# Opening of a decoder's first layer: four token tiles normed before the first projection, 512-token blocks, constants loaded later

## The chip, the cores and the metric

The kernel runs on one core of a Trainium2 chip. The metric is the device time of one execution in microseconds (us); lower is better. All arithmetic on the matrix engine that matters here is in a rounded 32-bit format (`float32r`): each operand is split into a high part and a low part, and a product is made of three matmuls (high by high, high by low, low by high).

## The reference

The reference is a two-layer decoder over 1024 tokens of width 1024. Layer 0 is gated linear attention followed by a squared-ReLU MLP; layer 1 is windowed attention with sinks and another MLP. What matters here is the opening of layer 0:

```python
def rmsnorm(x, g):
    y = x * lax.rsqrt(jnp.mean(x * x, axis=-1, keepdims=True) + EPS) * g

def gla_mixer(h, w_in, w_gk2, b_gk, g_onorm, w_out):
    proj = h @ w_in                       # q 512 | k 512 | v 1024 | gate 1024 | glr 16
    gk = log_sigmoid(glr @ w_gk2 + b_gk) / 16
    bcum = cumsum of gk inside chunks of 64 tokens
    q_t = q * exp(bcum); k_t = k * exp(-bcum); k_dec = k * exp(b_last - bcum)
    # per head (4 of them): causal product inside a chunk, running state between chunks,
    # norm, silu(gate), output projection
```

## The kernel before, in words

Tokens lie in eight tiles of 128 (`x0` to `x7`, 512 KB each), in two halves of four tiles. For each tile `scaled` (lines 169 to 179) squares it on ScalarE with a running sum, makes the reciprocal root of the mean (`rstd_of`, lines 132 to 142: a Ln and an Exp on ScalarE, four small operations on VectorE) and multiplies tile, root and gain on VectorE. `turn_tile` (lines 184 to 197) transposes the result in eight 128x128 pieces on TensorE into two PSUM banks, and empties these in four pairs: ScalarE casts 256 columns to the high part (`hna_hi`, line 196), VectorE subtracts to get the low part (`hna_lo`, line 197). `norm_tile` is both.

The opening for head 0 (lines 229 to 394) does the following. The loads go out on SyncE's queue in the order x0, the gain row `g_mix0`, x1, the two weight blocks of q and k (`wqk`), x2, x3, then the low-rank gate weights `glr_raw` and `gk2_raw`, the constants `b_gk` and `g_on`, and x4 to x7. The weight blocks, `glr_raw`, `gk2_raw` and x4 to x7 share three slots of one pool (`raw_block`), so a load waits until an earlier user of its slot is done. Tiles 0 and 1 are normed and turned, tiles 2 and 3 only scaled; then a loop goes over the tokens in four steps of 256: the gate projection (`glr_part`, lines 271 to 280), then for q and k by turns one tile of the next pair is turned and 24 matmuls of 256 columns are done (`qk_part`), and the pair after that is scaled. `Head.decay` (lines 294 to 313) makes the decay factors of one half out of the gate with one matmul, five exponentials or logarithms, a scan and four more VectorE operations; `q_out` and `k_out` apply them to the PSUM results of q and k. Then come the value and gate projection per tile (`vg_proj`, matmuls of 512 columns), the chunk products (`inner`), and the next heads.

Three constants of the second layer, `gq`, `gkv` and `sinks` (lines 982 to 987), and `neg_sinks` (line 1098) are written far down in the program but have no input to wait for. A scheduler orders each engine's instructions by a simulated timeline in which the order of the program is only a priority. An instruction whose inputs the simulation takes as ready is put early. On the chip each engine then takes its instructions in that fixed order. `tc.issue_after(i)` adds an edge of order only: what the block traces on the engine of `i` is queued behind `i` on that engine. Engines other than that of `i` get no edge.

Of the kernel before, what the change touches and what calls it, by code (L numbers as in the profile page):

```python
# [16 lines left out]
P = 128  # L17
# [34 lines left out]
def kernel(  # L52
# [35 lines left out]
    def raw_block(shape, name):  # L88
        return raws.tile(shape, F32, tag="raw", name=name)
# [10 lines left out]
    def bank(tag, name, shape=None):  # L100
        return psum.tile(shape or [P, HALF], F32, tag=tag, name=name)
# [67 lines left out]
    def scaled(h, gain, name):  # L169

        hs = act_block([P, D], f"{name}_hs")
        ss = stat(f"{name}_ss", 1)
        nc.scalar.activation(hs, h, AF.Square, accum_out=ss)
        r = rstd_of(ss, D, name)
        if gain is None:
            nc.scalar.activation(hs, h, AF.Copy, scale=r)
        else:
            last["scaled"] = nc.vector.scalar_tensor_tensor(hs, h, r, gain, ALU.mult, ALU.mult)
        return hs
# [44 lines left out]

    def x_load(t, alloc):
        x_in[t] = alloc([P, D], f"x{t}")
        nc.sync.dma_start(x_in[t], xv[t * P:(t + 1) * P, :])

    x_load(0, act_block)
    g_mix0 = gain_rows(ln_mix[0], "g_mix0")  # L230
    x_load(1, act_block)

    def x_norm(t):
        norm_tile(hn, t, x_in[t], g_mix0, "na")
# [2 lines left out]
        return [load_cols(w_in, c + h * P, c + (h + 1) * P, f"wqk{h}_{c}") for c in (0, 512)]  # L237

    raw_qk = qk_load(0)
    for t in range(2, 4):  # L240
        x_load(t, act_block)

    gla_ctx = ExitStack()
    small = gla_ctx.enter_context(tc.tile_pool(name="gla", bufs=3))
    glr_raw = raw_block([P, KD, 16], "glr_raw")
    nc.sync.dma_start(glr_raw, w_in[:, 3072:3088].rearrange("(k p) c -> p k c", p=P))
    glr_w = small.tile([P, KD, 32], F32R, name="glr_w", bufs=1)
    gk2_raw = raw_block([32, 512], "gk2_raw")
    for i in range(2):
        nc.sync.dma_start(gk2_raw[i * 16:(i + 1) * 16, :], a_w_gk2[0])  # L250
    gk2 = small.tile([P, 512], F32R, name="gk2", bufs=1)
    glrT = act_block([P, T], "glrT", F32R)
    b_gk = small.tile([P, GLA_HEADS], F32, name="b_gk", bufs=1)
    nc.sync.dma_start(b_gk, a_b_gk[0].rearrange("(h p) -> p h", p=P), allow_slow_non_contiguous=True)
    g_on = small.tile([P, 256], F32, name="g_on", bufs=1)
    nc.sync.dma_start(g_on, a_onorm[0].partition_broadcast(P))

    not_first = small.tile([P, HALF], U8, name="not_first", bufs=1)
    nc.gpsimd.memset(not_first, 1)
    nc.gpsimd.memset(not_first.rearrange("p (c j) -> p c j", j=CHUNK)[:, :, 0:1], 0)  # L260
# [96 lines left out]
    nc.gpsimd.memset(gk2[96:P, :].bitcast(F32), 0.0)  # L357
    nc.gpsimd.memset(glrT[96:P, :].bitcast(F32), 0.0)
    for t in range(4, NT):
        x_load(t, raw_block)  # L360
    x_norm(0)
    x_norm(1)
    nc.scalar.copy(glr_w[:, :, 0:16], glr_raw)
    nc.vector.tensor_sub(glr_w[:, :, 16:32], glr_raw, glr_w[:, :, 0:16].bitcast(F32))
    for r in (0, 32):
        nc.scalar.copy(gk2[r:r + 32, :], gk2_raw)
    nc.vector.tensor_sub(gk2[64:96, :], gk2_raw, gk2[0:32, :].bitcast(F32))
    head = Head(0)
    qkw = qk_split(0, raw_qk)
    hs = {t: scaled(x_in[t], g_mix0, f"na{t}") for t in (2, 3)}  # L370
    ps_qk = []
    for half in range(2):
        ps_qk.append([bank("mm", f"q0_{half}"), bank("sc", f"k0_{half}")])
        for i in range(2):
            c0, c1 = i * 256, (i + 1) * 256
            t = 4 * half + 2 * i + 2
            glr_part(half, c0, c1)
            if t == NT:
                head.decay(1)
            for j in range(2):  # L380
                if t + j < NT:
                    turn_tile(hn, t + j, hs[t + j], "na")
                qk_part(ps_qk[half][j], qkw[j], half, c0, c1)
            for j in range(2):
                if t + j + 2 < NT:
                    hs[t + j + 2] = scaled(x_in[t + j + 2], g_mix0, f"na{t + j + 2}")
            if t + 2 >= NT:
                g = (t + 2 - NT) // 2
                if g == 0:
                    head.decay(0)  # L390
                head.q_out(g, ps_qk[g][0])
                head.k_out(g, ps_qk[g][1])
    for w in qkw:
        wt.back(*w)

# [15 lines left out]
    for h in range(GLA_HEADS):  # L411
        qt, kt, kd = head.e
        ebl = head.ebl
        if h > 0:
# [4 lines left out]
                    fin(half, ps)  # L419
            for w in qkw:  # L420
                wt.back(*w)
        wvg = vg_weights(h)
        pair = "p (n e j) -> p n e j"
        qp = act_block([P, T], f"qp{h}", F32R)
        ql = act_block([P, T], f"ql{h}", F32R)
# [16 lines left out]
        if h + 1 < GLA_HEADS:  # L442
            head = Head(h + 1)
            for half in range(2):
                head.decay(half)
            qkw = qk_split(h + 1, qk_load(h + 1))
        else:
            wo = proj_weights(a_w_out[0], "wo", 0, 3, (0,))

# [18 lines left out]
        def inner(n, v, sg):  # L468
            e = slice(n * P, n * P + CHUNK)
            o = slice(n * P + CHUNK, (n + 1) * P)  # L470
            ps = bank("sc", f"at{h}_{n}", [P, P])
            matmul(ps[:, 0:CHUNK], lhsT=kt[:, n * P:(n + 1) * P], rhs=qt[:, e], start=True, stop=True)
            matmul(ps[0:CHUNK, CHUNK:P], lhsT=kd[:, e], rhs=qt[:, o], start=True, stop=True)
            matmul(ps[CHUNK:P, CHUNK:P], lhsT=kt[:, o], rhs=qt[:, o], start=True, stop=True)
            at = attn_sb[n % 2]
            nc.vector.copy_predicated(at, causal.bitcast(U32), ps)
            ah = small.tile([P, 2, P], F32R, tag="at", name=f"ah{h}_{n}", bufs=1)
            nc.scalar.copy(ah[:, 0], at)
            nc.vector.tensor_sub(ah[:, 1], at, ah[:, 0].bitcast(F32))
# [23 lines left out]
            nc.vector.scalar_tensor_tensor(o_out, po, r, sg, ALU.mult, ALU.mult)  # L503

        prev = vg_proj(0)
        kn = [act_block([P, NT, P], f"kn{h}_{i}", F32R) for i in range(2)]
# [38 lines left out]
    class Blocks:  # L545
# [35 lines left out]
        def second_half(self, units, hs):  # L581
# [37 lines left out]
            for p1, p2, hi, lo, r11, b12, t1, b22 in work:  # L619
# [2 lines left out]
                nc.scalar.copy(hi["t4"], p2)  # L622
                v.tensor_sub(lo["t4"], p2, hi["t4"].bitcast(F32))

    def mix_out(first, lhs_of, wo, res_of, gain, name, mlp, begun=()):
        nxt = first
        hs = {}
        for t in range(NT):
            if t < len(begun):
                ht = begun[t]  # L630
            else:
                ht = act_block([P, D], f"{name}h{t}")
                nc.sync.dma_start(ht, res_of(t))
            lhs = nxt
            if t + 1 < NT:
                nxt = lhs_of(t + 1)
            if t == 6:
                mlp.blocks.second_half([(0, 0)], hs)
            proj_tile(lhs, wo, ht, f"{name}{t}", (range(K_BEGUN, KD),) if t < len(begun) else K_ALL)
            nc.sync.dma_start(mlp.h_in[t * P:(t + 1) * P, :], ht)  # L640
# [338 lines left out]
    mix_out(og_first, og_split, wo, lambda t: xv[t * P:(t + 1) * P, :], g_mlp0, "op", mlp)  # L979


    gq = const.tile([P, KD, 1], F32, name="gq")
    nc.sync.dma_start(gq, ln_mix[1].rearrange("(k p o) -> p k o", p=P, o=1), allow_slow_non_contiguous=True)
    gkv = const.tile([P, KD, 1], F32, name="gkv")
    nc.sync.dma_start(gkv, kv_norm.rearrange("(k p o) -> p k o", p=P, o=1), allow_slow_non_contiguous=True)
    sinks = const.tile([P, HEADS, 1], F32, name="sinks")
    nc.sync.dma_start(sinks, b_sinks[0].rearrange("(h o) -> h o", o=1).partition_broadcast(P))

    def gained(w, c0, c1, g, name, alloc=wt_block):
        raw = load_cols(w, c0, c1, name)  # L990
# [104 lines left out]
    oT = [act_block([P, KD, P], f"oT{t}") for t in range(NT)]  # L1095

    neg_sinks = const.tile([P, HEADS, 1], F32, name="neg_sinks")
    nc.vector.tensor_scalar(neg_sinks, sinks, -1.0, None, ALU.mult)

    UNIT = 2  # L1100
    STEPS = NT * NT
# [217 lines left out]
```

## Time and profile before

| what | value |
|---|---|
| median of 3 runs | 2114.4 us (2110.25 to 2116.42) |
| the profiled execution, its own time | 2115.71 us |
| its span in the trace | 2114.0 us |
| mean granted TensorE clock over the span | 0.985 of full speed |
| TensorE matmul busy | 2007.2 us (95%) |
| VectorE / ScalarE / GpSimd busy | 1567.2 / 970.0 / 241.9 us |

PE is TensorE, PEld its weight loads, DVE is VectorE, ACT is ScalarE, POOL is GpSimd, SP is SyncE and SPq the DMA issues of its queue. Matmuls overlap each other in the pipe, so the pace of a run of matmuls is read from start to start, not from the duration of one. "Idle" is the time for which an engine stood still just before an instruction, and the name behind the arrow is what let it go on. About 1.7 us of the execution's time lie outside the span.

### The profile page before, as it was taken

How to read it: one execution, taken by the hardware profiler on the slowest of the kernel's cores; microseconds unless marked ns; L12 is line 12 of the kernel's file. 1: busy time of each engine (PE TensorE's matmuls, PEld its weight loads, DVE VectorE, ACT ScalarE, POOL GpSimd, SP SyncE). 2: the span in 40 equal slices, each digit the busy share in tenths (PEclk: the TensorE clock that was granted, in tenths of full speed). 3: DMA queues.
4: the chain of work that ended last, by engine and by line, in shares of the span. 5: the costliest groups of instructions: out<-in, count | busy, mean ns of one | idle time of the engine just before them, and what ended most of it. 6: DMA issues, size and time to landing. Idle time of an engine off the chain costs nothing. (4 is left out here: it accounts for less than half of the span.)

```text
span 2114.0 us, 27260 instructions
## 1 busy us (share of the span) xinstructions
PE 2007.2 (95%) x9498; PEld 1662.1 (79%) x9498; DVE 1567.2 (74%) x3075; ACT 970.0 (46%) x2104; POOL 241.9 (11%) x252
## 2 busy tenths in 40 slices
PE   5899999997999999999988999998999999999996
PEld 5788888886788888888876778777788888888885
DVE  5767766658877768877885788866877776877786
ACT  5534433435555544333345577744554454433333
POOL 2231322101000000000010334422000000000000
PEclk9999999998999999999999999999999999999999
DMA  5216211421665569955321111222456567955502
GB/s 146 60 35 86 60 40 31 132 88 50 215 203 193 179 235 379 337 191 207 111 74 56 36 31 46 101 80 70 140 196 203 199 204 283 412 216 209 189 11 100
DMA packets 176809, 308.26 MB, mean 146 GB/s; under 512 B 14176, under 2 KB 110592, under 8 KB 176672
## 3 DMA queue, kind: packets, MB, share of 16 engines
q1 hardware_dynamic: 176672, 306.52, 42.8%
q8 instruction: 75, 1.23, 0.2%
q14 instruction: 62, 0.51, 0.1%
HBM read 202.67 MB, written 103.81 MB: 145 GB/s over the span
## 5 line engine op out<-in xcount | busy, mean ns | idle before, releaser
L106 PE MATMUL dx<-dt,ds 128*128 128x512 f32 x672 | 154.9, 389 | 0.6 <-ACT dt L684 0.6
L106 PEld LDWEIGHTS dx<-dt,ds 128*128 128x128 f32 x672 | 125.9, 188 | 27.6 <-ACT dt L684 1.4
L875 DVE TENSOR_TENSOR hr<-hr,dx 128x512 f32<-128x512 f32 x160 | 107.9, 681 | 37.7 <-PE dx L106 37.2
L684 ACT CAST ds<-du 128x512 fp32r<-128x512 f32 x128 | 79.2, 619 | 119.7 <-PE dy L106 51.7
L684 ACT CAST s<-s 128x512 fp32r<-128x512 f32 x128 | 79.5, 621 | 101.3 <-PE ux L106 50.3
L685 DVE TENSOR_TENSOR s<-s,s 128x512 fp32r<-128x512 f32 x128 | 87.8, 689 | 48.4 <-ACT s L684 48.3
L684 ACT CAST db<-dw 128x512 fp32r<-128x512 f32 x96 | 55.7, 619 | 122.7 <-PE dx L106 46.5
L106 PE MATMUL vg<-wvg_hi,hna_hi 128*128 128x512 f32 x256 | 102.9, 402 | 5.4 <-DVE e L318 4.8
L106 PE MATMUL vg<-wvg_hi,hna_lo 128*128 128x512 f32 x256 | 101.9, 398 | 0.0
L106 PE MATMUL vg<-wvg_lo,hna_hi 128*128 128x512 f32 x256 | 101.5, 397 | 0.0
L685 DVE TENSOR_TENSOR ds<-du,ds 128x512 fp32r<-128x512 f32 x128 | 90.7, 710 | 7.9 <-ACT ds L684 7.9
L106 PE MATMUL ux<-hb_t4h,a 128*128 128x512 f32 x256 | 86.5, 399 | 8.0 <-DVE u L761 7.9
L106 PE MATMUL dz<-db,da 128*128 128x512 f32 x384 | 93.9, 389 | 0.0
L106 PE MATMUL uz<-hb_b21h,a 128*128 128x512 f32 x256 | 88.3, 407 | 4.1 <-DVE u L733 4.1
L684 ACT CAST a<-wu 128x512 fp32r<-128x512 f32 x96 | 58.8, 620 | 62.1 <-PE uy L106 46.1
L106 PE MATMUL uy<-hb_b22h,s 128*128 128x512 f32 x256 | 85.0, 389 | 0.0
L106 PE MATMUL ux<-hb_b11h,a 128*128 128x512 f32 x256 | 84.3, 390 | 0.0
L106 PE MATMUL uy<-hb_t1h,s 128*128 128x512 f32 x256 | 84.3, 390 | 0.0
L106 PEld LDWEIGHTS dz<-db,da 128*128 128x128 f32 x384 | 72.0, 188 | 15.3 <-DMA da<-uo 0.3
L106 PE MATMUL ux<-hb_t3h,s 128*128 128x512 f32 x256 | 84.0, 389 | 0.0
L106 PE MATMUL ux<-hb_t2h,s 128*128 128x512 f32 x256 | 84.0, 389 | 0.0
L106 PE MATMUL dx<-db,da 128*128 128x512 f32 x336 | 79.6, 389 | 0.0
(390 smaller groups left out, 5627.2 us busy)
## 6 DMA issues: line engine op xcount, KB each, us to landing
uo<-uo SPq DMA_DIRECT2D x96, 512.0 KB, 5.1
da<-uo SPq DMA_DIRECT2D x96, 512.0 KB, 6.4
wu<-in_w_up_dram SPq DMA_DIRECT2D x64, 512.0 KB, 4.6
dw<-in_w_down_dram SPq DMA_DIRECT2D x64, 512.0 KB, 5.5
du<-us SPq DMA_DIRECT2D x64, 512.0 KB, 7.0
us<-us SPq DMA_DIRECT2D x32, 512.0 KB, 2.7
us<-u SPq DMA_DIRECT2D x64, 256.0 KB, 5.4
wvg_raw<-in_a_w_in_dram SPq DMA_DIRECT2D x32, 256.0 KB, 3.0
```

The lines of the kernel that those rows point to most:

```text
L106: ins = nc.tensor.matmul(*args, **kw)
L684: nc.scalar.copy(op[:, 0], src)
L685: nc.vector.tensor_sub(op[:, 1], src, op[:, 0].bitcast(F32))
L875: nc.vector.tensor_add(h, h, ps)
```

## The change

It loads x0 to x3 before the two weight blocks, and puts x4 to x7 and the gate weights into the 36-slot pool of activations instead of the three slots; `b_gk` and `g_on` are loaded after x7. It norms and turns tiles 0 to 3 before the first projection; the casts of the gate weights and of the q and k weights stand behind the last Square of these four on ScalarE. The gate projection and q and k of head 0 are done 512 tokens at a time. After the projections of half 0 tiles 4 to 7 are normed, with the `gk2` casts behind the Square of tile 4, and the casts of the v and gate weights of every head stand behind the Square of tile 5. The q and k weights of the next heads are loaded behind x7 on SyncE's queue. The three constants of the second layer are loaded behind the first store of the output projection, and `neg_sinks` stands behind the last operation of the gated attention on VectorE.

```diff
-        nc.scalar.activation(hs, h, AF.Square, accum_out=ss)
+        last["square"] = nc.scalar.activation(hs, h, AF.Square, accum_out=ss)
...
     x_load(0, act_block)
     g_mix0 = gain_rows(ln_mix[0], "g_mix0")
-    x_load(1, act_block)
+    for t in range(1, 4):
+        x_load(t, act_block)
...
     raw_qk = qk_load(0)
-    for t in range(2, 4):
-        x_load(t, act_block)
...
-    glr_raw = raw_block([P, KD, 16], "glr_raw")
+    gl_raw = act_block([P, D], "gl_raw")
+    glr_raw, gk2_raw = gl_raw[:, 0:KD * 16].rearrange("p (k c) -> p k c", k=KD), gl_raw[:32, HALF:D]
...
     for t in range(4, NT):
-        x_load(t, raw_block)
-    x_norm(0)
-    x_norm(1)
-    nc.scalar.copy(glr_w[:, :, 0:16], glr_raw)
-    nc.vector.tensor_sub(glr_w[:, :, 16:32], glr_raw, glr_w[:, :, 0:16].bitcast(F32))
-    for r in (0, 32):
-        nc.scalar.copy(gk2[r:r + 32, :], gk2_raw)
-    nc.vector.tensor_sub(gk2[64:96, :], gk2_raw, gk2[0:32, :].bitcast(F32))
+        x_last = x_load(t, act_block)
+    b_gk = small.tile([P, GLA_HEADS], F32, name="b_gk", bufs=1)
+    nc.sync.dma_start(b_gk, a_b_gk[0].rearrange("(h p) -> p h", p=P), allow_slow_non_contiguous=True)
+    g_on = small.tile([P, 256], F32, name="g_on", bufs=1)
+    nc.sync.dma_start(g_on, a_onorm[0].partition_broadcast(P))
+    for t in range(2):
+        x_norm(t)
+    for t in range(2, 4):
+        x_norm(t)
+    with tc.issue_after(last["square"].ins):
+        nc.scalar.copy(glr_w[:, :, 0:16], glr_raw)
+        nc.vector.tensor_sub(glr_w[:, :, 16:32], glr_raw, glr_w[:, :, 0:16].bitcast(F32))
+        qkw = qk_split(0, raw_qk)
     head = Head(0)
-    qkw = qk_split(0, raw_qk)
-    hs = {t: scaled(x_in[t], g_mix0, f"na{t}") for t in (2, 3)}
     ps_qk = []
     for half in range(2):
+        glr_part(half, 0, HALF)
         ps_qk.append([bank("mm", f"q0_{half}"), bank("sc", f"k0_{half}")])
-        for i in range(2):
...
+        for ps, w in zip(ps_qk[half], qkw):
+            qk_part(ps, w, half, 0, HALF)
+        if half == 0:
+            for t in range(4, NT):
+                x_norm(t)
+                if t == 4:
+                    with tc.issue_after(last["square"].ins):
+                        for r in (0, 32):
+                            nc.scalar.copy(gk2[r:r + 32, :], gk2_raw)
+                        nc.vector.tensor_sub(gk2[64:96, :], gk2_raw, gk2[0:32, :].bitcast(F32))
+                if t == 5:
+                    square = last["square"]
+        head.decay(half)
+        head.q_out(half, ps_qk[half][0])
+        head.k_out(half, ps_qk[half][1])
...
-        wvg = vg_weights(h)
+        with tc.issue_after(square.ins):
+            wvg = vg_weights(h)
...
-            qkw = qk_split(h + 1, qk_load(h + 1))
+            with tc.issue_after(x_last.ins):
+                raw_next = qk_load(h + 1)
+            qkw = qk_split(h + 1, raw_next)
...
+            first_store.setdefault(name, nc.sync.dma_start(mlp.h_in[t * P:(t + 1) * P, :], ht))
...
+    with tc.issue_after(first_store["op"].ins):
+        gq = const.tile([P, KD, 1], F32, name="gq")
+        nc.sync.dma_start(gq, ln_mix[1].rearrange("(k p o) -> p k o", p=P, o=1), allow_slow_non_contiguous=True)
...
...
-    nc.vector.tensor_scalar(neg_sinks, sinks, -1.0, None, ALU.mult)
+    with tc.issue_after(last["gla"].ins):
+        nc.vector.tensor_scalar(neg_sinks, sinks, -1.0, None, ALU.mult)
```

## Rows read from the trace of the kernel before

**Rows 1.** The page's first part: busy time of each engine, its share of the span, and instructions.
```profile
PE 2007.2 (95%) x9498; PEld 1662.1 (79%) x9498; DVE 1567.2 (74%) x3075; ACT 970.0 (46%) x2104; POOL 241.9 (11%) x252
```

**Rows 2.** The table by stretches: stretch (us from the span's start) and its length, busy time of PE, PEld, DVE, ACT and POOL with instructions in brackets, granted clock of TensorE, share of the DMA engines, GB/s.
```profile
0.00:23.00 23.00, 3.61 (x16) 3.14 (x16) 7.80 (x22) 11.71 (x25) 8.08 (x16) 1.00 0.84 239
23.00:54.00 31.00, 29.14 (x233) 27.34 (x232) 20.07 (x48) 18.12 (x48) 4.80 (x2) 1.00 0.27 81
...
54.50:58.50 4.00, 0.00 (x0) 0.00 (x0) 3.96 (x5) 3.11 (x8) 1.97 (x1) 1.00 0.03 10
58.50:64.00 5.50, 5.47 (x17) 4.34 (x18) 3.60 (x8) 1.58 (x4) 2.82 (x1) 0.69 0.93 258
...
76.00:115.00 39.00, 34.18 (x171) 27.90 (x171) 31.77 (x67) 20.70 (x54) 8.11 (x7) 0.91 0.09 28
...
98.00:112.00 14.00, 10.50 (x49) 8.32 (x48) 11.38 (x32) 4.94 (x18) 1.42 (x2) 0.76 0.00 1
...
115.00:200.00 85.00, 84.94 (x430) 70.45 (x429) 63.85 (x135) 33.50 (x94) 24.90 (x17) 1.00 0.45 75
...
400.00:500.00 100.00, 93.46 (x465) 78.68 (x464) 56.15 (x108) 41.92 (x101) 9.19 (x8) 0.97 0.26 85
```

**Rows 3.** The timeline of TensorE in the opening: start us, duration us, engine, line, operation, what it writes and reads, shape, count, and in brackets the idle time before it. `na_tp` are transposes of a normed tile, `glr_ps` the gate projection, `q` and `k` the projections, `vg` the value and gate projection.
```profile
21.33 1.94 PE L111 MATMUL na_tp<-ident,na_hs 128*128 128x128 f32 x8 [11.05 <-DVE na_v L136]
...
23.07 0.42 PE L106 MATMUL glr_ps<-hna_hi,glr_w 128*32 128x256 f32 x1
...
58.53 0.50 PE L106 MATMUL vg<-wvg_hi,hna_hi 128*128 128x512 f32 x1 [4.06 <-DVE e L318]
```

**Rows 4.** The timelines of ScalarE and VectorE between 9 and 20 us, same columns.
```profile
9.60 1.04 ACT L123 CAST wqk_hi<-wqk_raw 128x1024 fp32r<-128x1024 f32 x1 [3.35 <-DMA wqk_raw<-in_a_w_in_dram]
...
11.38 1.04 ACT L123 CAST wqk_hi<-wqk_raw 128x1024 fp32r<-128x1024 f32 x1 [0.47 <-DMA wqk_raw<-in_a_w_in_dram]
...
13.79 1.06 ACT L173 ACTIVATE na_hs<-x 128x1024 f32<-128x1024 f32 x1
...
17.34 0.17 DVE L1098 TENSOR_SCALAR neg_sinks<-sinks 128x16 f32<-128x16 f32 x1 [2.21 <-DMA sinks<-in_b_sinks_dram]
...
17.75 1.26 ACT L366 CAST gk<-gk_raw 32x512 fp32r<-32x512 f32 x2 [2.38 <-DMA gk_raw<-in_a_w_gk_dram]
19.03 0.20 ACT L138 ACTIVATE na_r<-na_r 128x1 f32<-128x1 f32 x1
```

**Rows 5.** The timeline of SyncE's queue: start, time that the issue held the queue, line, what is loaded.
```profile
11.02 0.89 SPq L983 DMA_DIRECT2D gq<-in_ln_mix_dram  x1
11.96 2.03 SPq L985 DMA_DIRECT2D gkv<-in_kv_norm_dram  x1
14.03 0.98 SPq L987 DMA_DIRECT2D sinks<-in_b_sinks_dram  x1
...
16.04 13.36 SPq L227 DMA_DIRECT2D x<-in_x_dram  x4
```

**Rows 6.** Groups of VectorE's, then of ScalarE's instructions in the first 60 us, by shape: busy us, mean ns of one, and idle time before them.
```profile
L178 DVE SCALAR_TENSOR_TENSOR na_hs<-x,na_r,g_mix 128x1024 f32<-128x1024 f32 x8 | 10.3, 1284 | 0.3
L197 DVE TENSOR_TENSOR hna_lo<-na_tp,hna_hi 128x256 fp32r<-128x256 f32 x25 | 10.2, 420 | 12.8 <-ACT hna_hi L196 12.7
L306 DVE TENSOR_TENSOR_SCAN e<-not_first,e 128x512 f32<-128x512 uint8 x1 | 1.2, 1225 | 0.0
L318 DVE SCALAR_TENSOR_TENSOR e<-q,e 128x512 f32<-128x512 f32 x1 | 0.7, 684 | 0.0
L196 ACT CAST hna_hi<-na_tp 128x256 fp32r<-128x256 f32 x26 | 9.3, 368 | 4.9 <-DVE hna_lo L197 3.2 <-PE na_tp L111 1.6
L173 ACT ACTIVATE na_hs<-x 128x1024 f32<-128x1024 f32 x8 | 8.4, 1052 | 2.4 <-DMA x<-in_x_dram 2.4
```

**Rows 7.** VectorE's small steps for tile 0 from the timeline: first row at which it starts, last at which the scaled tile begins; with the second and third row they are the four small steps of one tile.
```profile
5.62 0.15 DVE L136 TENSOR_SCALAR na_v<-na_ss 128x1 f32<-128x1 f32 x1 [5.62 <-ACT na_hs L173]
6.28 0.22 DVE L139 SCALAR_TENSOR_TENSOR na_t<-na_r,na_v 128x1 f32<-128x1 f32 x1 [0.51 <-ACT na_r L138]
6.53 0.15 DVE L140 TENSOR_SCALAR na_t<-na_t 128x1 f32<-128x1 f32 x1
6.71 0.16 DVE L141 TENSOR_TENSOR na_r<-na_r,na_t 128x1 f32<-128x1 f32 x1
```

**Rows 8.** Pace of TensorE, from its timeline, start to start: 256 columns (first and last of ten matmuls in a row), four transposes and what follows them, 512 columns of head 1 (first and last of eleven), and 512 columns at 60 us, two in a row.
```profile
28.04 0.28 PE L106 MATMUL q<-hna_lo,wqk_hi 128*128 128x256 f32 x1
...
29.11 0.28 PE L106 MATMUL q<-hna_lo,wqk_hi 128*128 128x256 f32 x1
...
51.57 0.60 PE L111 MATMUL na_tp<-ident,na_hs 128*128 128x128 f32 x4
51.93 0.36 PE L106 MATMUL k<-hna_hi,wqk_hi 128*128 128x256 f32 x1
...
150.17 0.39 PE L106 MATMUL mmqk<-hna_lo,wqk_hi 128*128 128x512 f32 x1
...
152.43 0.39 PE L106 MATMUL mmqk<-hna_hi,wqk_lo 128*128 128x512 f32 x1
...
60.26 0.63 PE L106 MATMUL vg<-wvg_hi,hna_hi 128*128 128x512 f32 x1
60.69 0.63 PE L106 MATMUL vg<-wvg_lo,hna_hi 128*128 128x512 f32 x1
```

More of the change, by code (lines that the diff above doesn't have):

```diff
@@ L226, in x_load @@
         x_in[t] = alloc([P, D], f"x{t}")
-        nc.sync.dma_start(x_in[t], xv[t * P:(t + 1) * P, :])
+        return nc.sync.dma_start(x_in[t], xv[t * P:(t + 1) * P, :])
     x_load(0, act_block)
     g_mix0 = gain_rows(ln_mix[0], "g_mix0")
-    x_load(1, act_block)
+    for t in range(1, 4):
+        x_load(t, act_block)
     def x_norm(t):
@@ L239 @@
     raw_qk = qk_load(0)
-    for t in range(2, 4):
-        x_load(t, act_block)
     gla_ctx = ExitStack()
     small = gla_ctx.enter_context(tc.tile_pool(name="gla", bufs=3))
-    glr_raw = raw_block([P, KD, 16], "glr_raw")
+    gl_raw = act_block([P, D], "gl_raw")
+    glr_raw, gk2_raw = gl_raw[:, 0:KD * 16].rearrange("p (k c) -> p k c", k=KD), gl_raw[:32, HALF:D]
     nc.sync.dma_start(glr_raw, w_in[:, 3072:3088].rearrange("(k p) c -> p k c", p=P))
     glr_w = small.tile([P, KD, 32], F32R, name="glr_w", bufs=1)
-    gk2_raw = raw_block([32, 512], "gk2_raw")
     for i in range(2):
@@ L252 @@
     glrT = act_block([P, T], "glrT", F32R)
[L253 to L256, printed above, removed]
     not_first = small.tile([P, HALF], U8, name="not_first", bufs=1)
@@ L371 @@
     ps_qk = []
     for half in range(2):
+        glr_part(half, 0, HALF)
         ps_qk.append([bank("mm", f"q0_{half}"), bank("sc", f"k0_{half}")])
-        for i in range(2):
[L375 to L392, printed above, removed]
+        for ps, w in zip(ps_qk[half], qkw):
+            qk_part(ps, w, half, 0, HALF)
@@ L502, in inner @@
             r = rstd_of(ss, 256, f"on{h}_{n}")
-            nc.vector.scalar_tensor_tensor(o_out, po, r, sg, ALU.mult, ALU.mult)
+            last["gla"] = nc.vector.scalar_tensor_tensor(o_out, po, r, sg, ALU.mult, ALU.mult)
         prev = vg_proj(0)
@@ L623, in second_half @@
                 v.tensor_sub(lo["t4"], p2, hi["t4"].bitcast(F32))
+    first_store = {}
     def mix_out(first, lhs_of, wo, res_of, gain, name, mlp, begun=()):
@@ L639, in mix_out @@
             proj_tile(lhs, wo, ht, f"{name}{t}", (range(K_BEGUN, KD),) if t < len(begun) else K_ALL)
-            nc.sync.dma_start(mlp.h_in[t * P:(t + 1) * P, :], ht)
+            first_store.setdefault(name, nc.sync.dma_start(mlp.h_in[t * P:(t + 1) * P, :], ht))
             hs[t] = scaled(ht, gain, f"{name}n{t}")
@@ L979 @@
     mix_out(og_first, og_split, wo, lambda t: xv[t * P:(t + 1) * P, :], g_mlp0, "op", mlp)
[L982 to L987, printed above, removed]
+    with tc.issue_after(first_store["op"].ins):
+        gq = const.tile([P, KD, 1], F32, name="gq")
+        nc.sync.dma_start(gq, ln_mix[1].rearrange("(k p o) -> p k o", p=P, o=1), allow_slow_non_contiguous=True)
+        gkv = const.tile([P, KD, 1], F32, name="gkv")
+        nc.sync.dma_start(gkv, kv_norm.rearrange("(k p o) -> p k o", p=P, o=1), allow_slow_non_contiguous=True)
+        sinks = const.tile([P, HEADS, 1], F32, name="sinks")
+        nc.sync.dma_start(sinks, b_sinks[0].rearrange("(h o) -> h o", o=1).partition_broadcast(P))
     def gained(w, c0, c1, g, name, alloc=wt_block):
```

## The prediction, as it was put on record

> **What bounds the kernel now.** I read the page's first part for the engine that carries the kernel, then the table by stretches for where that engine is not carried, then the timelines of those stretches. TensorE is busy 95% of the span [rows 1]. The table shows where the other 5% lie that this change can reach: from 115 to 200 us TensorE has next to no idle time, at full clock, but in the first 23 us it works 3.6 us, from 54.5 to 58.5 us not at all, and from 76 to 115 us it lacks 4.8 us [rows 2]. Behind the opening TensorE is full, so what is won or lost ahead of that point moves everything behind it by as much, at first sight to the end. The opening is therefore priced by when TensorE has done the same work.
>
> **Why the opening is slow.** The dense run starts at 23.07, after transposes of tile 1 that waited 11.05 us [rows 3]. The reader should see a queue in the wrong order. Tile 1 is squared only at 13.79, behind the casts of the q and k weights (the second at 11.38, let go by its load). Its Exp stands at 19.03 behind the `gk2` casts, for whose load ScalarE stood still 2.38 us; VectorE at the same time stood 2.21 us at `neg_sinks` for the load of `sinks` [rows 4]. SyncE's queue spends 3.9 us on `gq`, `gkv` and `sinks`, which nobody needs for hundreds of us, ahead of `gk2_raw` and x4, and the four last tiles then go out over 13.4 us as slots come free [rows 5].
>
> **The change part by part.**
>
> *Start of the dense run: 2.1 us earlier.* The five loads x0, `g_mix0`, x1, x2, x3 are now the first five. Before, the fourth and the fifth load released their readers at 9.60 and 11.38, 1.8 us apart [rows 4], so x3 is there at about 11.4. VectorE needs per tile the four small steps 0.68, the scaling 1.28 and four subtractions of 0.42, in all 3.64 us; ScalarE a Square of 1.05, its accumulator and Ln and Exp of 0.6, and four casts of 0.37, in all 3.1 us [rows 6, 7]. VectorE is the longer lane. It starts at 5.6 and has 2 us of work until tile 0 is turned at about 10. What then remains of four tiles is 14.6 - 2.0 = 12.6 us, so all is done at about 22.6. The projection can begin when the first of the last tile's four pieces is out, some 1.3 us earlier: 21.3, and I take 21.0, as such subtractions start closer than they last. Ends: 19.5 if VectorE is dense from 9 us, 24 if the Squares of x2 and x3 are put ahead of tile 0's casts and VectorE stands until 12.
>
> *Transposes already done: 1.4 us.* Tiles 2 and 3 are turned before the dense run instead of within it: 16 transposes at 0.36 us per four [rows 8].
>
> *512 columns instead of 256: 1.1 us.* 192 matmuls for q and k become 96. Ten of 256 columns take 1.07 us in nine steps, 0.119 each; ten steps of 512 columns 2.26 us, 0.226 each [rows 8]. 96 x (0.238 - 0.226) = 1.1 us; the gate projection I leave at nothing, bounded by the same 0.012 on its 32 pairs, 0.4 us. The Trainium skill, page "TensorE: Matmul & The Clock Gate", section "Back-to-back issue gap", puts a fixed 2.5 ns on top of the columns of each matmul; by it the term would be an estimated 0.24 us, as the loads of weights stand outside that formula. The rows decide.
>
> *Stalls inside the opening: 7.6 us.* Between 23 and 54 TensorE lacks 1.9 us, from 54.5 to 58.5 it lacks 4.06 (it waits for q's factors behind the late tiles 6 and 7), and in the 5.5 us behind that the granted clock is 0.69, a loss of 1.7 [rows 2, 3]; two matmuls there start 0.43 us apart against 0.226 [rows 8]. These follow from x4 to x7 coming late and in pieces [rows 5]; with them in the 36-slot pool they are issued at once and have landed by about 24 us, six large loads behind x3 at 1.8 us each, and the small ones. All three go, if tiles 4 to 7 are normed under the projections of half 0.
>
> *What comes in its place: 2.0 us lost.* Half 0 has 16 + 48 matmuls of 0.226, 14.5 us, and 32 transposes, 2.9 us, so TensorE is covered until 21.0 + 17.4 = 38.4. Tiles 4 to 7 take VectorE 14.6 us from 22.6, with 1.1 for gate results and weights: 38.3. That cover is just enough. If the scheduler puts the decay of half 0 between (a scan of 1.2, three operations of 0.68, one for q and two for k of 0.68, some 5.3 us in all [rows 6]), TensorE waits for tile 7. I take 1.5 of that, ends 0 and 5.3. The first 512-column matmuls run at half clock as the first 256-column ones do now (0.42 us for one against 0.28 [rows 3, 8]); with a little more work in that stretch I take 0.5, ends 0 and 1.7 (the loss at 58.5 us).
>
> *Edits at nothing.* The q and k weights land two loads later, at about 13 and 15 instead of 9.6 and 11.4 (two loads of 1.8 us); their split is needed only behind the gate projection, 3.6 us after the start. Were that cover gone, the price is the second split's lateness, at most 3 us. `b_gk` and `g_on` go behind x7 to some 26 us; the first decay is due later than that. The v and gate weights get their slots earlier than before. The three constants cost SyncE 3.9 us where the output projection stores its tiles [rows 5]. TensorE is short of work there anyway for 6.5 of 100 us [rows 2], SyncE has one load and one store per tile, and the constants have no reader for hundreds of us. Bounds: 0.5 us won, 3.9 lost. `neg_sinks` could hold VectorE for its load once more, 2.2 us as now [rows 4], but behind the gated attention VectorE has gaps. I take 0.
>
> *The stretch behind, 76 to 115 us: 0.* It loses 4.8 us idle and some 3.4 by clock (14 us at 0.76 [rows 2]). Its waits are for VectorE, with the decays of heads 0 and 1 heaped up. The new order moves half 0's decay ahead, but the same work of head 1 follows. I leave it, ends 8 us won (all goes) and 4 us lost.
>
> *Sum.* 2.1 + 1.4 + 1.1 + 7.6 - 2.0 = 10.2 us off. The profiled execution took 2115.7, its span 2114.0; that gives 2105.5. This execution lies 1.3 us above the median of the runs, so by the median it would be 2104.2. I say 2105. A measurement of this kernel can tell about 0.3%, 6.3 us, from no change: faster means under 2108.1, slower over 2120.7.
>
> **Rivals.**
>
> *The later stretch goes too.* With half 0's decay, q and k done some 20 us ahead of half 1's, VectorE has less heaped up at head 1, and the stall of 2.7 us with its half clock goes. For it: VectorE is busy only 20 of 31 us from 23 to 54, so there is room [rows 2]. Against it: the stall is a chain of state and chunk products, not the heap alone. Time: 2105 - 8 = 2097.
>
> *VectorE becomes the bound of the opening.* The two lanes have four tiles to do before anything starts and four more under half 0, and the casts and subtractions already wait for each other (12.7 us of VectorE's idle is for ScalarE's casts [rows 6]). The scheduler's order holds edges on ScalarE only; VectorE, SyncE and TensorE may be put otherwise than the program says, so that the change does not do all it says. With the start at 24 (3.0 lost), the full 5.3 us before tile 7 (3.8 more than taken), 1.2 more at half clock: 10.2 - 8.0 = 2.2 us off, 2113.5.
>
> *Slower: nothing overlaps between the halves.* TensorE now has no 256-token step to fall back on. If VectorE does decay, q and k of half 0 first and norms tiles 4 to 7 only then, half 0 ends at 24 + 15 = 39, the outputs at 41, tile 7 at 41 + 15 = 56, half 1 at 56 + 15 + 1.7 = 72.7. Before, that work less the 5.4 us of `vg` for tile 0, done in between, ended at about 70.5. So 2.2 us are lost, and if the heads behind inherit the order with another 4 us, 2122. It decides against the change from the point where tile 7 is turned later than 54 us. Against it: tiles 4 to 7 stand ahead of the decay in the program, and VectorE works only two thirds of this stretch today [rows 2].
>
> **How the numbers follow.** Forecast 0.52 (2100 to 2110), later stretch too 0.14, VectorE bound 0.22, slower 0.12. The range takes 2095 to 2115: the low end holds most of the first rival, the high end the whole of the second. Faster by over 0.3%: nearly all of the forecast's 0.52 (0.48) and the first rival, 0.62. Slower by over 0.3%: 0.09, the slower rival's upper part and mishaps far behind the opening. Same: 0.29.
>
> **What would show it.** In the changed profile: first gate projection at 21 (19.5 to 24) with four tiles turned; Squares of tiles 0 to 3 ahead of the weight casts on ScalarE; no wait for `gk2_raw` or `sinks` before 40 us; x7 issued before 20 us; q and k of half 1 done by about 56 to 58 us; no gap like that of 4.06 us. Wrong would be: a start after 24, a gap of more than 5 us between the two halves, a gap on TensorE near the constants' loads, or an order of heads 1 to 3 that loses more than 4 us where TensorE is full today.

## The result and the profile after

The changed kernel takes 2131.4 us (median; 2131.2 to 2134.2), beside 2113.9 for the kernel before on the same chip: a ratio of 1.009, interval 1.0076 to 1.0104. It is 17.5 us **slower**, where 2105 and "faster" were forecast. The profiled execution took 2134.2 us, its span 2132.5.

The table by stretches of the changed kernel, columns as in [rows 2]; the third and fifth stretch were not shown before.
```profile
0.00:23.00 23.00, 4.97 (x20) 3.85 (x20) 10.86 (x27) 13.66 (x32) 7.71 (x16) 1.00 0.93 291
23.00:54.00 31.00, 20.54 (x85) 14.91 (x85) 11.51 (x26) 11.30 (x26) 4.08 (x3) 0.94 0.11 32
46.00:72.00 26.00, 6.89 (x31) 5.14 (x30) 18.37 (x34) 14.78 (x34) 9.30 (x4) 0.58 0.28 81
54.00:76.00 22.00, 9.70 (x37) 7.66 (x38) 17.44 (x32) 9.83 (x26) 5.58 (x3) 0.54 0.31 94
76.00:115.00 39.00, 35.90 (x167) 27.98 (x166) 22.02 (x39) 18.84 (x38) 8.49 (x5) 0.91 0.09 27
115.00:200.00 85.00, 83.31 (x429) 69.23 (x427) 65.42 (x136) 33.58 (x93) 24.60 (x17) 1.00 0.31 51
```
Against [rows 2] TensorE has lost 8.6 us of work between 23 and 54 (29.14 to 20.54). A new hole stands between 46 and 72: 6.89 us of work in 26, at a granted clock of 0.58. Behind 76 us the stretches look as before. The last q and k matmul of head 3 starts at 320.55 before and at 338.25 after: at 320 us the whole loss (17.7) is there, and it is only carried on.

TensorE in the opening, columns as in [rows 3]:
```profile
15.99 1.94 PE L111 MATMUL na_tp<-ident,na_hs 128*128 128x128 f32 x8 [5.42 <-DVE na_v L136]
21.55 1.08 PE L111 MATMUL na_tp<-ident,na_hs 128*128 128x128 f32 x4 [3.61 <-DVE na_t L140]
26.07 2.28 PE L111 MATMUL na_tp<-ident,na_hs 128*128 128x128 f32 x8 [3.44 <-DVE hna_lo L197]
...
28.81 0.64 PE L106 MATMUL glr_ps<-hna_hi,glr_w 128*32 128x512 f32 x1 [0.46 <-ACT hna_hi L196]
...
46.11 0.40 PE L106 MATMUL k<-hna_hi,wqk_lo 128*128 128x512 f32 x1
46.35 0.60 PE L111 MATMUL na_tp<-ident,na_hs 128*128 128x128 f32 x4
...
58.45 1.94 PE L111 MATMUL na_tp<-ident,na_hs 128*128 128x128 f32 x8 [11.26 <-DVE na_v L136]
...
63.41 1.09 PE L111 MATMUL na_tp<-ident,na_hs 128*128 128x128 f32 x4 [3.03 <-DVE hna_lo L197]
...
70.41 2.02 PE L111 MATMUL na_tp<-ident,na_hs 128*128 128x128 f32 x8 [4.47 <-DVE hna_lo L197]
72.08 0.78 PE L106 MATMUL glr_ps<-hna_hi,glr_w 128*32 128x512 f32 x1
```
Two things are to be seen. The first gate projection starts at 28.81, not at 21.0 (at 23.07 before, [rows 3]). And half 0's last k matmul starts at 46.11, while tile 5 is turned at 58.45, tile 6 at 63.4 and tile 7 at 70.4: the second half of tile 4 and all of tiles 5 to 7 are turned behind half 0's projections, not under them. Half 1's first gate projection starts at 72.08.

ScalarE, same columns: the Squares (L173) and what stands ahead of them.
```profile
11.82 0.37 ACT L196 CAST hna_hi<-na_tp 128x256 fp32r<-128x256 f32 x1 [0.55 <-DVE hna_lo L197]
12.09 1.06 ACT L173 ACTIVATE na_hs<-x 128x1024 f32<-128x1024 f32 x1
...
17.52 1.99 ACT L123 CAST wqk_hi<-wqk_raw 128x1024 fp32r<-128x1024 f32 x2
19.41 0.64 ACT L196 CAST hna_hi<-na_tp 128x256 fp32r<-128x256 f32 x2
...
46.98 0.37 ACT L196 CAST hna_hi<-na_tp 128x256 fp32r<-128x256 f32 x1 [4.06 <-PE na_tp L111]
47.84 0.37 ACT L196 CAST hna_hi<-na_tp 128x256 fp32r<-128x256 f32 x1 [0.49 <-DVE hna_lo L197]
48.12 1.06 ACT L173 ACTIVATE na_hs<-x 128x1024 f32<-128x1024 f32 x1
...
49.16 2.92 ACT L123 CAST wvg_hi<-wvg_raw 128x1024 fp32r<-128x1024 f32 x3
```
The Square of x1 (12.09) stands behind the last cast of tile 0, and the Square of x5 (48.12) behind the last cast of tile 4. Tile 4's last casts wait for its transposes at 46.35, and those stand on TensorE behind half 0's last k matmul. So tile 5 is squared only when half 0 is done, and three v and g casts stand between its Square and its Ln.

VectorE in the changed kernel:
```profile
21.50 1.87 DVE L141 TENSOR_TENSOR na_r<-na_r,na_t 128x1 f32<-128x1 f32 x1
...
52.90 2.03 DVE L141 TENSOR_TENSOR na_r<-na_r,na_t 128x1 f32<-128x1 f32 x1
54.97 3.33 DVE L178 SCALAR_TENSOR_TENSOR na_hs<-x,na_r,g_mix 128x1024 f32<-128x1024 f32 x1
```
GpSimd at those times:
```profile
18.70 4.65 POOL L124 TENSOR_TENSOR wqk_lo<-wqk_raw,wqk_hi 128x1024 fp32r<-128x1024 f32 x2 [14.48 <-ACT wqk_hi L123]
50.27 6.94 POOL L124 TENSOR_TENSOR wvg_lo<-wvg_raw,wvg_hi 128x1024 fp32r<-128x1024 f32 x3 [26.92 <-ACT wvg_hi L123]
```
One small step takes 0.16 us in [rows 7] and 1.87 and 2.03 here, the scaling 1.28 in [rows 6] and 3.33 here. The step of 21.50 ends at 23.37, GpSimd's pair of subtractions at 23.35. In the hole this adds up: from the start of x5's Square (48.12) to the end of its scaling are 10.2 us, against 3.8 in a run where neither casts nor subtractions stand between (e2, 48.03 to 51.79; the same gap there is 4.84). So some 6.4 us of the first gap, 11.26, belong to the v and g casts and to GpSimd.

### The profile page after: what moved, and what is told of

The parts are those of the page before. It is cut to its first block, busy times and chain, and to the rows that moved or that the text cites. A ratio compares the mean times of both kernels' runs of the same rounds, so it can differ in the third digit from the quotient of the medians.

```text
span 2132.5 us, 26997 instructions
## 1 busy us (share of the span) xinstructions
PE 2013.4 (94%) x9370; PEld 1659.1 (78%) x9370; DVE 1571.5 (74%) x3073; ACT 969.0 (45%) x2100; POOL 241.2 (11%) x252
```

## The experiments

Each ran beside the kernel before on the same chip (2114 to 2116 us). The changed kernel has the ratio 1.009. Not all ran on one chip, so two rows are better compared by their ratios than by their medians, which can differ by 2 or 3 us on that account.

| kernel | us | ratio to before, interval |
|---|---|---|
| e1 Squares of tiles 4 to 7 ahead | 2127.9 | 1.0061, 1.0040 to 1.0083 |
| e2 v and g casts later | 2133.6 | 1.0094, 1.0074 to 1.0114 |
| e3 Squares of tiles 0 to 3 ahead | 2135.6 | 1.0099, 1.0081 to 1.0118 |
| e4 loads alone, on before | 2118.8 | 1.0018, 1.0009 to 1.0027 |
| e5 tiles 4 to 7 turned between | 2104.6 | 0.9956, 0.9944 to 0.9969 |
| e6 no low parts of weights | 2130.2 | 1.0080, 1.0055 to 1.0105 |
| e7 e4 with v and g held | 2113.3 | 1.0002, 0.9989 to 1.0014 |
| e8 constants alone, on before | 2112.3 | 0.9993, 0.9980 to 1.0006 |
| e9 e5 with the turning behind | 2114.7 | 1.0000, 0.9991 to 1.0009 |
| e10 turning between, alone | 2123.2 | 1.0042, 1.0026 to 1.0058 |
| e11 e5 with the first four too | 2103.3 | 0.9950, 0.9933 to 0.9967 |
| e12 e11 with the last four held | 2106.7 | 0.9962, 0.9950 to 0.9974 |

**e1, the Squares of tiles 4 to 7 ahead.**
```diff
             for t in range(4, NT):
-                x_norm(t)
+                hs[t] = scaled(x_in[t], g_mix0, f"na{t}")
...
+            with tc.issue_after(last["square"].ins):
+                for t in range(4, NT):
+                    turn_tile(hn, t, hs[t], "na")
```


> The changed kernel, but tiles 4 to 7 are all scaled before any of them is turned, and the casts of their turning stand behind the Square of x7 on ScalarE. Theory A (queue order: the Squares of x5 to x7 stand behind tile 4's casts, which wait for TensorE's transposes behind k of half 0): the hole from 47 to 70 us on TensorE closes for the most part, 12 to 18 us off the 2131.4 of the changed kernel, 2113 to 2119. Theory B (the hole is made by the three casts of the v and g weights and by GpSimd's subtractions, which hold VectorE): under 4 us off, 2127 to 2132, since both still stand behind the Square of x5.

2127.9. By the median that lies at the lower end of theory B's range (3.5 us off); by the ratios it is about 6 us off, between the two. The Squares of x5 to x7 came at 25.6, 30.5 and 37.6. But the v and g casts hang on the Square of x5 and came with it, and the dense run began only at 36.95. The hole stayed, smaller:
```profile
52.83 1.03 PE L111 MATMUL na_tp<-ident,na_hs 128*128 128x128 f32 x8
55.30 0.63 PE L111 MATMUL na_tp<-ident,na_hs 128*128 128x128 f32 x4 [1.20 <-DVE hna_lo L197]
...
58.20 1.09 PE L111 MATMUL na_tp<-ident,na_hs 128*128 128x128 f32 x4 [1.07 <-DVE hna_lo L197]
...
63.84 1.09 PE L111 MATMUL na_tp<-ident,na_hs 128*128 128x128 f32 x4 [3.02 <-DVE hna_lo L197]
```
These transposes had their scaled tiles by 43 us, yet they stand on TensorE behind half 0's last k matmul (52.60). From there each pair of transposes waits for the casts and subtractions of the pair ahead, with half 0's decay among them on VectorE, until 65.8. That made a new theory (D): what is exposed is the place of the turning in TensorE's own order.

**e2, the v and g casts later**, behind the Square of x7 in place of x5's (`if t == 7: square = last["square"]`).

> The changed kernel, but the casts of the v and g weights stand behind the Square of x7 instead of that of x5. Theory A: only the part of the hole that the casts and GpSimd's subtractions add goes: 2.9 us of casts between the Square and the Ln of x5, and 1.9 + 2.0 us by which VectorE's last small step and scaling of x5 outlast the same operations elsewhere (2.03 against 0.16, 3.33 against 1.28): 4 to 7 us off, 2124 to 2127.5. Theory B: most of the hole goes, 12 us or more off, under 2119.

2133.6: both missed, nothing is gained. Tile 5 is turned at 51.94 instead of 58.45, but the same casts and GpSimd's subtractions now fall among tiles 6 and 7, and the last wait is 7.96 us instead of 4.47.

**e3, the Squares of tiles 0 to 3 ahead.**
```diff
-    for t in range(2):
-        x_norm(t)
-    for t in range(2, 4):
-        x_norm(t)
+    hs = {t: scaled(x_in[t], g_mix0, f"na{t}") for t in range(4)}
+    with tc.issue_after(last["square"].ins):
+        for t in range(4):
+            turn_tile(hn, t, hs[t], "na")
```


> The changed kernel, but tiles 0 to 3 are all scaled before any is turned, and the casts of their turning stand behind the Square of x3. Theory A, applied to the start (the Square of x1 at 12.09 stands behind tile 0's casts although x1 is there at about 8): the first gate projection moves from 28.8 to 22 to 25 us, 4 to 7 us off, 2124 to 2127; the hole behind half 0 stays. Theory C (the start is bound by the work of ScalarE and VectorE on four tiles, whatever their order): within 2 us of 2131.4.

2135.6, no gain. Three tiles were scaled by 14.1, but then the casts of `glr_w` (which waited 1.22 us for its load) and of the q and k weights stood ahead of tile 0's later casts; the start came at 29.9 and the hole as before. What stands ahead had only changed its name.

**e4, the loads alone**: the kernel before with the changed order of loads, the input tiles in the 36-slot pool and the constants late; the 256-token steps kept.

> The kernel before with the loads of the change alone: x0 to x3 ahead of the weights, x4 to x7 and the gate weights in the 36-slot pool, the constants of both layers late; the steps of 256 tokens and the order of the norms stay. If the late loads made the stalls of the opening, as the prediction had it: 4 to 10 us off the 2113.9 of the kernel before, 2104 to 2110. If queue order made them: within 3 us of 2113.9.

2118.8: slower than before, outside both forecasts. x7 was issued by 14.3 and the gap of 4.06 of [rows 3] was gone, but the second transposes came at 23.71 and the dense run stuttered until 34.68. The v and g weights now came early too: their casts stood at 24.7, 27.0 and 28.8, GpSimd's subtractions from 25.8 to 32.8.

**e5, the turning between the quarters of half 0's projection**: the Squares as in e1, the v and g casts held behind tile 7's last cast.
```diff
-        for ps, w in zip(ps_qk[half], qkw):
-            qk_part(ps, w, half, 0, HALF)
...
+        pinned["PE"] = half == 0
+        for i, (ps, w) in enumerate(zip(ps_qk[half], qkw)):
+            for j in range(2):
+                qk_part(ps, w, half, 0, HALF, range(4 * j, 4 * j + 4))
+                if half == 0:
+                    turn_tile(hn, 4 + 2 * i + j, hs[4 + 2 * i + j], "na")
+        pinned["PE"] = False
+        if half == 0:
+            square = last["cast"]
```


> The changed kernel with tiles 4 to 7 all scaled before any of them is turned (as in e1), the turning of tiles 4, 5, 6 and 7 fixed on TensorE behind the first half of q, the second half of q, the first half of k and the second half of k of half 0, and the first head's v and g casts held behind the last cast of tile 7. In e1 TensorE finished half 0 at 52.6 and reached the first gate projection of half 1 at 65.8. Theory D (the order of TensorE puts the turning of tiles 4 to 7, sixteen casts and subtractions of about 0.86 us, behind half 0's projections): that gap shrinks to under 4 us, and with the start back at about 30 instead of 32 the time is 2112 to 2118. Theory C (ScalarE and VectorE have this much work wherever it stands, the opening is bound by them): the projection of half 0 is stretched by what the gap loses, 2124 to 2130.

2104.6, 7 us under the lower end of theory D and 26.9 better than the changed kernel (28 by the ratios); it beats the kernel before by 0.31 to 0.56%. Its table by stretches, then its TensorE:
```profile
23.00:54.00 31.00, 25.46 (x119) 18.00 (x120) 23.14 (x56) 16.45 (x47) 0.34 (x1) 1.00 0.10 30
54.00:76.00 22.00, 22.00 (x103) 16.84 (x102) 7.02 (x13) 12.02 (x20) 14.30 (x7) 1.00 0.50 144
76.00:115.00 39.00, 37.54 (x204) 31.34 (x203) 34.42 (x80) 19.00 (x58) 7.09 (x7) 1.00 0.00 1
...
98.00:112.00 14.00, 14.00 (x79) 11.91 (x78) 10.30 (x29) 5.18 (x21) 1.73 (x3) 1.00 0.00 1
```
```profile
30.59 0.78 PE L106 MATMUL glr_ps<-hna_hi,glr_w 128*32 128x512 f32 x1
...
39.37 1.03 PE L111 MATMUL na_tp<-ident,na_hs 128*128 128x128 f32 x8
...
50.36 0.39 PE L106 MATMUL k<-hna_hi,wqk_lo 128*128 128x512 f32 x1
51.09 0.63 PE L111 MATMUL na_tp<-ident,na_hs 128*128 128x128 f32 x4 [0.35 <-DVE hna_lo L197]
52.18 0.42 PE L106 MATMUL glr_ps<-hna_hi,glr_w 128*32 128x512 f32 x1 [0.46 <-ACT hna_hi L196]
```
Half 0's last k matmul starts at 50.36 and half 1's first gate projection at 52.18: 1.8 us between the halves, where the changed kernel has 26.0 (46.11 to 72.08). It starts 1.8 us later than the changed kernel and has half 1's last k matmul at 68.19 instead of 91.09. From 54 to 76 TensorE has no idle time, and its clock is full. Against the kernel before, though, the opening itself wins nothing: the last v and gate matmul of tile 3 starts at 98.35, before at 97.42. That of tile 7 starts at 126.50, before at 133.93. So what e5 has won by then, 7.4 us, it wins between these two points, where the kernel before works 10.50 of 14 us at a clock of 0.76 [rows 2] and e5 all 14.00 at full clock.

**e6, without the low parts of the first head's weights** (GpSimd's six subtractions left out, the high parts in their place).

> The changed kernel without GpSimd's six subtractions for the low parts of the first head's q, k, v and g weights (the high parts are used in their place, so the low parts are left out of the product; the matmuls stay as many). Theory E (while GpSimd subtracts 1024 columns, VectorE's operations from SBUF to SBUF are held, 0.16 us steps took 1.9 to 2.0 and a 1.28 us scaling 3.3): the first gate projection comes 2 to 3 us before 28.8 and tile 7 is turned 3 to 4 us sooner, 2124 to 2128. If what holds the tiles back is the order on ScalarE and TensorE alone: within 2 us of 2131.4.

2130.2, within 2 us of the changed kernel, as the second case had it; but the trace bears theory E out at the start. The first gate projection comes at 26.74 instead of 28.81, and the small step of tile 3 takes what it took in [rows 7] (its line is two further down here):
```profile
21.14 0.16 DVE L143 TENSOR_TENSOR na_r<-na_r,na_t 128x1 f32<-128x1 f32 x1
...
52.35 1.94 PE L111 MATMUL na_tp<-ident,na_hs 128*128 128x128 f32 x8 [7.35 <-DVE na_v L138]
62.96 1.94 PE L111 MATMUL na_tp<-ident,na_hs 128*128 128x128 f32 x8 [8.67 <-DVE hna_lo L199]
```
But the 2.1 us ahead run into the same hole. Tile 5 is turned after a gap of 7.35 instead of 11.26; then the next head's subtractions come in (GpSimd from 55.4 to 63.7), and tile 6 waits 8.67. So this run does not free the hole of subtractions, and what they cost there it does not tell.

**e7, e4 with the v and g casts held** behind tile 7's last cast.

> e4 (before, with the loads in the changed order, the input tiles in the activations' pool and the constants late; 256-token steps in the order of before) with the first head's v and g casts held behind the last cast of tile 7. e4 gave 2118.8 and had three of these casts and 7 us of GpSimd's subtractions between 24.7 and 32.8. Theory E and crowding (early loads let this work fall into the opening): 2110 to 2115. If the order of the Squares and weight casts (second transposes at 23.7) is what counts: within 2 us of 2118.8.

2113.3, 5.5 us better than e4 by the medians and 3.4 by the ratios, whose intervals overlap: the casts and subtractions that early loads had let into the opening are probably what e4 lost. The second transposes still came at 23.80, and against the kernel before nothing is gained (1.0002).

**e8, the constants alone**, on the kernel before.

> Before, with only the four constants of the second mixer (gq, gkv, sinks and their negative) loaded and worked out later. All theories: these do not sit on the path that sets the end, apart from 3 to 4 us of the SP queue ahead of input tiles 4 to 7 (11.02 to 16.04): 2111 to 2115, and not the place where the 17 us come from.

2112.3, no difference that can be told (0.9980 to 1.0006).

**e9, e5 with the turning put back** behind half 0's projection; Squares and held casts stay.

> e5 with the turning of tiles 4 to 7 put back behind half 0's last k matmul on TensorE; the Squares ahead and the v and g casts held behind tile 7's last cast stay as in e5. Theory D (the place of the turning on TensorE is what costs): sixteen casts and subtractions stand uncovered again behind half 0 (about 8 to 13 us), 2113 to 2120. If the held casts and the early Squares gave e5's 27 us: within 3 us of 2104.6.

2114.7, as theory D had it: 10.2 us more than e5, and the hole is back (half 0's last k matmul at 46.88):
```profile
47.11 1.03 PE L111 MATMUL na_tp<-ident,na_hs 128*128 128x128 f32 x8
...
54.02 1.09 PE L111 MATMUL na_tp<-ident,na_hs 128*128 128x128 f32 x4 [0.45 <-DVE hna_lo L197]
58.12 1.09 PE L111 MATMUL na_tp<-ident,na_hs 128*128 128x128 f32 x4 [3.02 <-DVE hna_lo L197]
...
60.12 0.78 PE L106 MATMUL glr_ps<-hna_hi,glr_w 128*32 128x512 f32 x1
```
From 47.1 to 60.1 are 13.0 us for sixteen casts with their subtractions. Not all of it is theirs: the wait of 3.02 is for VectorE, which does some 5.5 us of half 0's decay between 51.25 and 58.91.

**e10, the turning between alone**, with the Squares as in the changed kernel (the edit of e5 on TensorE's side, `x_norm(t)` in place of `turn_tile`).

> The changed kernel with the turning of tiles 4 to 7 fixed between the quarters of half 0's projection, and nothing else: Square x5 still stands behind tile 4's last cast on ScalarE and the v and g casts behind Square x5. Theory D alone: 2105 to 2112. If the place of the Squares counts as much (tile 5 is scaled only some 5 us after tile 4 is turned, and TensorE waits for it in the middle of q): 2115 to 2124. If neither: 2129 to 2133.

2123.2, the middle case: 8.2 us better than the changed kernel, and TensorE waits between q and k for tile 5:
```profile
51.12 1.94 PE L111 MATMUL na_tp<-ident,na_hs 128*128 128x128 f32 x8 [9.29 <-DVE na_v L136]
```
Its Square stands at 40.78, behind tile 4's last cast, but the scaling ends only at 50.97: here too the v and g casts and GpSimd's subtractions lie between, for 10.2 us instead of 3.8. The four kernels make a square: neither 2131.4, turning alone 2123.2, Squares and held casts alone (e9) 2114.7, both 2104.6. The two edits are worth 8.2 and 16.7 us each alone and 26.9 together (by the ratios some 10, 19 and 28). The second is itself two things. e1 has the Squares ahead without holding the casts (but for one edge of order on ScalarE) and takes 2127.9 against e9's 2114.7: with the Squares ahead, holding the casts is worth 13 us, and moving them alone (e2) nothing. Fixing TensorE's order for the turning fixes the gate projection ahead of q and q ahead of k as well; that was not tried apart.

**e11, e5 with the first four tiles done alike**: all Squares and scalings first, `glr_w` cast behind tile 1, the q and k weights behind tile 3, `gk2` behind the Square of x7.

> e5 with the same done for the first four tiles: all four Squares and scalings ahead of their casts, the cast of glr_w behind tile 1's last cast, those of the q and k weights behind tile 3's last, those of gk2 behind Square x7. In e5 the first gate projection came at 30.6, with VectorE's steps of tile 1 held from 21.5 to 23.4 while GpSimd subtracted q and k weights and two weight casts of 1 us ahead of tile 1's. If that order is what delays the start: it comes at 23 to 26 and the time is 2098 to 2101. If the sixteen casts and subtractions of 0.86 us bound the start in any order: 27 to 30 and 2102 to 2105.

2103.3, the best of all by its median, though not told apart from e5 (0.9933 to 0.9967 against 0.9944 to 0.9969). By start and time this is the second case, but e12 shows that its reason is not the one: the start came at 28.71 because the Squares of x4 to x7 (16.3, 18.0, 20.5, 23.1) now stood among the casts of tiles 1 to 3.

**e12, e11 with those Squares held** behind tile 3's last cast.

> e11 with the Squares and scalings of tiles 4 to 7 held behind tile 3's last cast (and the q and k weight casts) on ScalarE. In e11 the Squares of tiles 4 to 7 stood among the casts of tiles 1 to 3 (16.3 to 24.1) and the first gate projection came at 28.7. If that is what filled the start: it comes at 21 to 24, near the 21.0 of the forecast's first term, and the time is 2096 to 2101, as long as tile 4 is scaled before the first half of q is done (about 8.5 us behind the first gate projection). If the 0.86 us of a cast and its subtraction in turn bound the start: 26 to 29 and 2102 to 2105. If GpSimd's two subtractions of q and k weights then hold the scalings of tiles 4 to 7 and TensorE waits for them in the middle of q and k: a start of 21 to 24 with gaps of 2 to 5 us behind it, 2102 to 2106.

2106.7. The start came at 24.28, and what it won went into the gaps of the third case:
```profile
24.28 0.78 PE L106 MATMUL glr_ps<-hna_hi,glr_w 128*32 128x512 f32 x1
...
34.06 1.07 PE L111 MATMUL na_tp<-ident,na_hs 128*128 128x128 f32 x8 [1.28 <-DVE na_v L136]
...
39.83 0.47 PE L106 MATMUL z<-glrT,gk 128*128 128x512 f32 x1 [1.95 <-DVE gk L383]
41.14 0.63 PE L111 MATMUL na_tp<-ident,na_hs 128*128 128x128 f32 x4 [0.85 <-DVE hna_lo L197]
...
43.53 1.08 PE L111 MATMUL na_tp<-ident,na_hs 128*128 128x128 f32 x4 [1.76 <-DVE hna_lo L197]
```
The third case's cause is not what did it: GpSimd's pair ended at 31.7, and the scalings ran at 1.28 from 32.63 on. Tile 4's Ln stood at 31.27 on ScalarE, behind the casts of the gate result (30.09, which had waited 1.24 for the end of the gate projection), and the Squares of x5 to x7 behind it. Half 1's last k matmul starts at 69.40, against 68.19 in e5 and 65.64 in e11. A start 4 us earlier is worth nothing when the same work of tiles 4 to 7 is then late.

## Why the prediction was wrong, step by step

*What comes in its place, 2.0 us lost: this step failed, and it decides the sign.* I covered tiles 4 to 7 with half 0's projections by adding up what VectorE has to do (38.3 against 38.4) and asked only whether VectorE would take the decay first. I did not ask where the transposes of these tiles stand on TensorE. The diff puts `x_norm(4)` to `x_norm(7)` behind half 0's `qk_part`, where the kernel before had `turn_tile` ahead of each; in all runs with that order the last transposes of tiles 4 to 7 came behind the last k matmul, however early the tiles were scaled (e1, e9). On top of it the Square of x5 stood behind tile 4's last cast, and the v and g casts with GpSimd's subtractions behind that Square, in the hole. VectorE was idle under half 0, busy 11.51 of 31 us, instead of full. Where I had put 2.0 us, 26.0 lie between half 0's last k matmul (46.11) and half 1's first gate projection (72.08), and 1.8 in e5. e9 and e10 against e5 show both parts; together they hold more than the whole loss. The smaller share of this term was half clock, 0.5: ten steps of 0.43 from 28.81 on lose 2.0 us where the kernel before lost some 0.9, an estimated 1.1 (both from starts in the traces).

*The end on the slower side had the right point and the wrong mechanism.* "Tile 7 is turned later than 54 us" was its point, and 70.4 is far beyond it. It had VectorE's order as the cause and 2122 as the time. Half 0's decay did fall among tiles 6 and 7, but the hole begins at 46.35 on TensorE, before any decay. The forecast's own signs of being wrong were both there: a start after 24 and a gap of more than 5 us between the halves.

*Start of the dense run, 2.1 us earlier: 5.7 us later.* Two things failed. First the lane: I gave a tile's piece VectorE's 0.42 us, as if casts ran ahead. Rows such as 47.84 and many like it show the second cast of a bank starting 0.49 us behind the end of the first, let go by the first one's subtraction, so a piece costs up to 0.86 (46.98 to 47.84). Tile 0's four, with nothing else on the two engines, take 2.9 us (9.76 to 12.64) where I had 1.7; sixteen would be 11.5, at 0.86 each 13.8 us, and not 6.7. [rows 6] had said so: 12.7 us of VectorE's idle time for ScalarE's casts; I used them for a rival and not for the sum. e12, with nothing else ahead, starts at 24.28, just past my upper end. Second the order: the Square of x1 at 12.09, 2 us of weight casts ahead of tile 1's casts, and 2.1 us of VectorE held (e6).

*Edits at nothing.* Right for the constants (e8). Wrong for the q and k weights: I priced when their split is needed, not where its casts stand on ScalarE and what its subtractions do to VectorE.

*Stalls inside the opening, 7.6 us.* The cause I gave, x4 to x7 late and in pieces, is at most part of it; and the gain did not last. In the wait of 4.06 in the kernel before, a copy on VectorE is held by GpSimd's subtraction (54.11 to 56.46):
```profile
54.21 2.29 DVE L308 COPY bl<-e 128x8 f32<-128x8 f32 x1
```
Behind it come tile 7's scaling and then q's factors, for which TensorE waits. In e8 GpSimd subtracts only from 55.48 on: the same copy takes 0.17 us, and what is held is a later operation for which TensorE does not wait. So some 2.1 of the 4.06 us are GpSimd's. The stretch in the kernel before, then in e7 (those loads early) and e8 (x7 issued by 27.5 instead of 29.4):
```profile
54.00:76.00 22.00, 17.94 (x115) 15.79 (x115) 13.73 (x26) 9.69 (x23) 7.36 (x4) 0.92 0.28 81
...
54.00:76.00 22.00, 19.63 (x140) 16.72 (x138) 11.96 (x21) 10.87 (x21) 12.27 (x5) 1.00 0.34 95
...
54.00:76.00 22.00, 22.00 (x154) 19.96 (x153) 14.77 (x28) 12.61 (x26) 10.14 (x5) 1.00 0.31 89
```
In both the wait of 4.06 and the low clock behind it are gone, and the time is the same. What e7 won here it lost beside it: its dense run starts at 25.54 instead of 23.07, and at 78.45 TensorE waits 3.87 us for q's factors, whose scan took VectorE 3.27 us beside GpSimd's subtractions (1.22 in [rows 6]). In e5 these stalls are gone too, but its start at 30.59 has used them up.

*512 columns, 1.1 us, and the transposes ahead, 1.4.* The pace is as forecast: in e5 the q matmuls from 36.63 to 39.13 make eleven steps of 0.227. The time of these two terms was not tried apart. *The later stretch, 0*: in the changed kernel 35.90 us of work in 39 against 34.18, as near to nothing as forecast. In e5 it is not nothing: there the stall from 98 to 112 is gone, as the first rival had it, and that is all that e5 has won by 126 us. What makes it go was not tried.

That e5 takes 2104.6 does not make the forecast of 2105 right: it starts at 30.6, not 21, is level with the kernel before at 98 us, and gains behind that what the forecast had gained ahead of 64. That the numbers agree is luck.

## What to carry to other kernels

A cover has to be checked on the engine that is covered: work that feeds the next stage through TensorE (transposes) must stand among its matmuls, not behind them, and its first step (here a Square) ahead of the previous tile's last. When two engines take turns on one buffer, price the pair and not the longer lane. Early loads do no good by themselves: they also let work in that nobody needs yet (e4), and a stall that goes can come back at the next wait (e7). And a faster kernel should be followed from event to event: e5 wins 50 us behind the place where it was changed.

## What the hardware showed that I had not expected

While GpSimd subtracts 1024 columns in SBUF (2.3 us each), VectorE's operations with two SBUF inputs wait for its end: 0.16 us became 1.87 and 2.03, 1.28 became 3.33, and 0.16 again without the subtraction (e6, tile 3's step). A copy of 128x8 was held as well (2.29 in the kernel before, 0.17 in e8), and a scan (3.27 in e7, 1.22 in [rows 6]). Subtractions from PSUM kept their length (0.41 at 20.99, inside GpSimd's pair). The Trainium skill, page "SBUF — State Buffer", section "SBUF: two separate sides", says the same: a shared port pair is an exclusive lock, and a VectorE operation with two SBUF inputs blocks fully against a GpSimd operation that reads SBUF. The trace agrees; I had left it out of the prediction.

The hole cost clock as well: from 54 to 76 us TensorE was granted 0.54 in the changed kernel, behind gaps of 11.26, 3.03 and 4.47 us, and 1.00 in e5 without them.
